# A two-layer hybrid trunk on one core: output projection, second norm and first up-projection products written as one order in the FFN's pool

## The chip, the cores and the metric

One Trainium2 chip, one core of it in use. The metric is the device time of one execution in microseconds; three executions of the kernel before gave 2158.92, 2163.03 and 2165.88 us, median 2163.03.

## The reference

640 tokens (512 latent, 128 context) of width 1024 go through two layers in fp32. What the change touches is the place between the two sub-layers:

```python
merged = jnp.sum(gates * proj, axis=2)
mix = merged @ w_out
x = x + gt1 * mix
h = rmsnorm(x, g2n) * (1 + sc2) + sh2
u, val = jnp.split(h @ w_up, 2, axis=-1)
u = dwconv3(u, conv)
x = x + gt2 * ((jax.nn.gelu(u) * val) @ w_down)
```

`w_out` is 1024x1024, `w_up` 1024x5632, `w_down` 2816x1024; shift, scale and gate come from the conditioning vectors, one value per channel for latent and one for context tokens.

## The kernel before

Activations lie transposed: 128 channels on the partitions, 640 tokens along the free axis, in two chunks of 320 (256 latent and 64 context tokens each). Every fp32 factor is split into a rounded part (`hi`, a cast on ScalarE) and a remainder (`lo`, a subtraction on VectorE), and a product is the sum of three matmuls hi·hi, hi·lo, lo·hi. One matmul streams 320 columns.

**Stages and pools.** Each layer is a mixer stage and an FFN stage. Each opens a pool of its own in the same stretch of SBUF, with the tags laid one behind the other in the order of `PLACES` (L32); a tile of the new pool waits only for those tiles of the old one that lie at its addresses. In the mixer's pool the last tags are `pt`, `yc` and `vm`; in the FFN's, `hT` and `wd`.

**Mixer, end.** Three branches (L570) go over eight column blocks each. A block is 48 matmuls of the input projection, 24 of the branch's own, gate and sum on VectorE. In the last branch the sum is split into `yc` (hi) and `vm` (lo): L191. Behind each split `aside` (L562) queues one or two blocks of the modulation vectors (`mod_block`, L203): two loads of 256 KB each into `pt`, `kc` or `vca`, and four dot products on VectorE (L212) that use `yt` as scratch. The loads take `pt`, `kc`, `pt`, `vca` in turn. In layer 0 two such blocks stand behind the last split, in layer 1 one.

**Output projection** (L614, `project`, called at L1075 from inside the mixer's stage): eight blocks of 48 matmuls; a block's weights (512 KB) come by SyncE's queue into `raw` (three buffers) and are split (L168, L169) into `hi` and `lo`. The last three blocks run the first token chunk together and then the second, so that the first chunk's sum of squares (L223) and root (L237) can be taken meanwhile.

**FFN.** The up-projection multiplies 2x2 blocks with seven products instead of eight (`Up`, L752): product p needs combination p of the weight quarters and combination p of the four quarters of the normalized activations. `norm_quarters` (L696) makes all of the latter: pair by pair for the first chunk (`two`, giving products 1 and 2), then the second chunk with products 7 and 6, and at last 5, 3 and 4 (`one`). A pair is two VectorE products with the spread root (L704), one ScalarE and one POOL operation on the latent strips (L710, L708) and two POOL operations on the context strips (L711). Weight quarters are loaded by SyncE (L643, L644) and added up partly by an accumulating DMA that POOL issues (L645); `sums` (L677) does the rest.

**Order.** Products 1 and 2 of the first three up-projection blocks (72 matmuls, L899 to L903) and all of `norm_quarters` stand before the manual schedule: their order on the engines is the scheduler's. From L1017 on TensorE, VectorE and ScalarE run in the order in which the code is written: a list of products `pe`, and behind each slot the work that `at(slot, rank, ...)` put there. The first 15 slots are the other five products of blocks 0, 1 and 2 (180 matmuls); slot 15 is product 1 of block 3, from where each block takes seven products.

Of the kernel before, what the change touches and what calls it, by code (L numbers as in the profile page):

```python
# [59 lines left out]
def hybrid_kernel(ctx: ExitStack, tc: tile.TileContext, a):  # L60
# [635 lines left out]
    def norm_quarters(x, l, which, rb):  # L696

        rbs = rb + rstd(x, 1)

        def raw_pair(c, i):  # L700
            t = big("gs", NG)
            for j in range(2):
                k, o = 2 * i + j, t[:, j * HALF:(j + 1) * HALF]
                nc.vector.tensor_tensor(o, rbs[c][:, :HALF], x[k][:, c * HALF:(c + 1) * HALF], ALU.mult)  # L704
                sh = mod[l][:, (0, 3)[which] * 8 + k, :]
                sc = scale1[l][:, which, k, :]
# [5 lines left out]
            return t  # L712

        def two(t, i, p0, p1):
            hi, lo = (big("hA", 8, F32R) if p0 == 1 else big("hT", 20, F32R) for _ in range(2))
            split(t, hi, lo)
            for j, p in enumerate((p0, p1)):
                out[i][p] = (hi[:, j * HALF:(j + 1) * HALF], lo[:, j * HALF:(j + 1) * HALF])

        def one(src, i, p):  # L720
            t = big("hT", 20, F32R)
            split(src, t[:, :HALF], t[:, HALF:])
            out[i][p] = (t[:, :HALF], t[:, HALF:])

        out = [{} for _ in range(NP)]
        first = []
        for i in range(NP):
            first.append(raw_pair(0, i))
            two(first[i], i, 1, 2)
        second, x76 = [], []  # L730
        for i in range(NP):
            b11, b21 = first[i][:, :HALF], first[i][:, HALF:]
            second.append(raw_pair(1, i))
            b12, b22 = second[i][:, :HALF], second[i][:, HALF:]
            x76.append(big("gs", NG))
            x7, x6 = x76[i][:, :HALF], x76[i][:, HALF:]
            nc.vector.tensor_tensor(x7, b22, b12, ALU.subtract)
# [6 lines left out]
        for i in range(NP):  # L744
            one(second[i][:, HALF:], i, 3)
# [543 lines left out]
```

## Time and profile before

| | us |
|---|---|
| median of three runs | 2163.03 |
| profiled execution | 2161.66 |
| its span | 2159.9 |
| TensorE busy in the span | 2059.6 |
| VectorE busy | 1389.7 |
| ScalarE busy | 824.4 |
| GpSimd (POOL) busy | 160.2 |

The profiled execution's own time is 1.76 us above its span and 1.37 us below the median. All times in rows are microseconds from the span's start unless marked ns. PE is TensorE, DVE VectorE, ACT ScalarE, POOL GpSimd, SP the queue of SyncE. A row's bracket gives the idle time of the engine just before and what ended it. Matmuls overlap: the pitch from one start to the next is what counts, not a matmul's own duration. PEclk is the granted share of TensorE's full clock.

### The profile page before, as it was taken

Reading aid. Unit: us, or ns where it says so; the run is one execution under the profiler, and the core shown is the slowest. Engines: PE = TensorE matmul, PEld = TensorE weight load, DVE = VectorE, ACT = ScalarE, POOL = GpSimd, SP = SyncE. Lnnn points to the kernel's source line nnn. Section 1 sums busy time; section 2 is a strip of 40 time slices with the busy share of each in tenths; the row PEclk is TensorE's granted clock in tenths of the full one; section 3 lists DMA queues with packets and bytes.
Section 4 is the critical chain, followed back from the end, with each engine's and each line's share of the span. In section 5 each row is a group of like instructions: output and inputs, shape, how many; then the busy total and the mean of one; then the engine's idle time right before and its main releaser. Section 6 shows DMA issues by size and latency. Waiting matters only on the chain.

```text
span 2159.9 us, 34811 instructions
## 1 busy us (share of the span) xinstructions
PE 2059.6 (95%) x13752; PEld 1983.4 (92%) x13752; DVE 1389.7 (64%) x2923; ACT 824.4 (38%) x1329; POOL 160.2 (7%) x344
## 2 busy tenths in 40 slices
PE   6999999999977999999989999999999599999997
PEld 4987999999977999999979779999999599999997
DVE  4247458889767677667652664676664785858676
ACT  4245432222335444344442462222222452535352
POOL 1001000000031000000040100000000310101000
PEclk9999999999988999999999999999999799999998
DMA  8241335556524545354232422353442263535332
GB/s 299 74 128 55 107 105 167 170 178 197 176 59 122 132 111 141 89 142 112 74 121 82 120 85 91 119 170 132 136 144 97 67 163 93 158 103 132 100 99 79
DMA packets 104291, 266.08 MB, mean 123 GB/s; under 512 B 11328, under 2 KB 20800, under 8 KB 104128
## 3 DMA queue, kind: packets, MB, share of 16 engines
q1 hardware_dynamic: 92160, 240.79, 33.4%
q0 software_dynamic: 11968, 23.07, 6.9%
q8 instruction: 108, 1.77, 0.3%
q14 instruction: 55, 0.45, 0.1%
HBM read 252.80 MB, written 6.29 MB: 120 GB/s over the span
## 4 chain that ended last, share of the span: by engine, by line
PE 85%; DVE 8%; DMA 2%; POOL 2%; ACT 2%; issue 1%; SPq 0%; DVEq 0%; POOLq 0%; ACTq 0%
PE mm L182 30%; PE b L763 19%; PE b L875 11%; PE m L182 10%; PE b L182 3%; PE ps L763 3%; DMA raw<-in_w_up 1%; PE ps L452 1%; PE ps L463 1%; DVE lo L672 1%; PE m L442 1%; DVE yt L212 1%; DVE lo L169 1%; PE mm L1121 1%; PE mm L386 1%
## 5 line engine op out<-in xcount | busy, mean ns | idle before, releaser
L182 PE MATMUL mm<-h,hi 128*128 128x320 f32 x2272 | 364.7, 314 | 0.0
L182 PEld LDWEIGHTS mm<-h,hi 128*128 128x128 f32 x2272 | 341.9, 190 | 5.8 <-issue 2.4
L763 PE MATMUL b<-hT,hi 128*128 128x320 f32 x1760 | 306.9, 313 | 16.2 <-ACT hT L190 10.5
L168 ACT CAST hi<-raw 128x1024 fp32r<-128x1024 f32 x140 | 146.8, 1049 | 418.0 <-PE mm L182 262.7
L763 PEld LDWEIGHTS b<-hT,hi 128*128 128x128 f32 x1760 | 273.1, 190 | 18.3 <-ACT hT L190 11.4
L169 DVE TENSOR_TENSOR lo<-raw,hi 128x1024 fp32r<-128x1024 f32 x140 | 172.4, 1232 | 141.8 <-PE mm L182 47.9
L212 DVE SCALAR_TENSOR_TENSOR yt<-mraw,cond 128x512 f32<-128x512 f32 x320 | 220.4, 689 | 7.2
L669 ACT CAST hi<-raw 128x1024 fp32r<-128x1024 f32 (+1 forms) x176 | 164.2, 941 | 120.6 <-DVE raw L679 71.7
L672 DVE TENSOR_TENSOR lo<-raw,hi 128x1024 fp32r<-128x1024 f32 (+1 forms) x176 | 189.7, 1085 | 16.1 <-ACT hi L669 16.1
L182 PE MATMUL mm<-h,lo 128*128 128x320 f32 x1136 | 185.3, 312 | 0.0
L763 PE MATMUL b<-hT,lo 128*128 128x320 f32 x880 | 167.6, 313 | 15.1 <-DVE lo L672 15.1
L182 PEld LDWEIGHTS mm<-h,lo 128*128 128x128 f32 x1136 | 169.8, 188 | 2.9 <-issue 1.0
L875 PE MATMUL b<-gs,hi 128*128 128x320 f32 x1088 | 169.3, 309 | 0.0
L875 PEld LDWEIGHTS b<-gs,hi 128*128 128x128 f32 x1088 | 162.0, 188 | 0.0
L605 DVE SCALAR_TENSOR_TENSOR mx<-b,mod,mx 128x256 f32<-128x256 f32 (+1 forms) x256 | 80.5, 377 | 120.5 <-PE b L875 96.5
L763 PEld LDWEIGHTS b<-hT,lo 128*128 128x128 f32 x880 | 140.2, 191 | 16.3 <-DVE lo L672 16.3
L693 ACT COPY sn<-b 128x320 f32<-128x320 f32 x176 | 75.1, 427 | 123.7 <-PE b L763 123.7
L182 PE MATMUL m<-h,hi 128*128 128x320 f32 x672 | 106.7, 314 | 8.9 <-ACT hi L168 5.9
L182 PEld LDWEIGHTS m<-h,hi 128*128 128x128 f32 x672 | 100.9, 190 | 11.2 <-ACT hi L168 6.1
L645 POOL DMA_DIRECT2D raw<-in_w_up x44 | 53.1, 1206 | 683.0 <-DVE raw L679 298.8
L763 PE MATMUL b<-hA,hi 128*128 128x320 f32 x400 | 80.7, 328 | 22.8 <-ACT hi L669 16.6
L831 DVE SCALAR_TENSOR_TENSOR tmp<-tmp,vecs,tmp 128x642 f32<-128x642 f32 x88 | 77.9, 887 | 21.9 <-ACT tmp L826 17.4
(251 smaller groups left out, 3302.6 us busy)
## 6 DMA issues: line engine op xcount, KB each, us to landing
raw<-in_w_in SPq DMA_DIRECT2D x96, 512.0 KB, 3.5
mraw<-in_w_mod SPq DMA_DIRECT2D x160, 256.0 KB, 2.8
raw<-in_w_up SPq DMA_DIRECT2D x44, 768.0 KB, 5.4
raw<-in_w_up SPq DMA_DIRECT2D x48, 512.0 KB, 3.9
raw<-in_w_up POOLq DMA_DIRECT2D x44, 512.0 KB, 6.5
raw<-in_w_branch SPq DMA_DIRECT2D x24, 512.0 KB, 3.5
wd<-in_w_down SPq DMA_DIRECT2D x32, 384.0 KB, 3.2
wd<-in_w_down SPq DMA_DIRECT2D x32, 320.0 KB, 2.8
```

The costliest lines, as they stand in the source:

```text
L168: nc.scalar.copy(hi[:, :c1 - c0], raw[:, c0:c1])
L169: lows[0] = nc.vector.tensor_tensor(lo[:, :c1 - c0], raw[:, c0:c1], hi[:, :c1 - c0].bitcast(F32), ALU.subtract)
L182: nc.tensor.matmul(bank(ps, c)[:, :HALF], lhsT=w, rhs=v[:, c * HALF:(c + 1) * HALF], start=first, stop=last)
L212: nc.vector.scalar_tensor_tensor(scr[:, :512], raw, 1.0, cond[s][:, hf * 512:(hf + 1) * 512], ALU.mult, ALU.mult, accum_out=acc[:, s, hf:h ...
L605: ins = nc.vector.scalar_tensor_tensor(xv, ps[c][:, sl], gt[:, s:s + 1], xv, ALU.mult, ALU.add)
L645: nc.gpsimd.dma_start(raw[:, 1536:2560].rearrange("p (b n) -> p b n", b=2), src[:, 1536:2048].unsqueeze(1).to_broadcast([P, 2, 512]), accu ...
L669: nc.scalar.copy(view(hi), src)
L672: return lambda: nc.vector.tensor_tensor(view(lo), src, view(hi).bitcast(F32), ALU.subtract)
L693: nc.scalar.copy(t, src)
L763: nc.tensor.matmul(o, lhsT=self.ws.w[p][wi][:, k * P:(k + 1) * P], rhs=self.xt[k][p][xi], start=fresh and j == 0 and k == 0, stop=j == 2 a ...
L831: nc.vector.scalar_tensor_tensor(self.cv[:, inner], self.u[:, j:PADW - 2 + j], self.tap(j), self.cv[:, inner], ALU.mult, ALU.add)
L875: nc.tensor.matmul(self.ps[c][:, :HALF], lhsT=self.w[wi][:, k * P:(k + 1) * P], rhs=self.ups[k].g[xi][:, c * HALF:(c + 1) * HALF], start=k ...
```

## The change

The output projection leaves the mixer's stage: `mixer` returns the merged activations and x, and `entry`, called inside the FFN's manual schedule, runs everything from the projection's first block to product 2 of block 2 in one written order. That schedule now also holds POOL. `yc` and `vm` move to the lasting pool, since the projection reads them in the FFN's stage; `hT` shrinks from 20 to 3 buffers, and the up-projection's split activations use `yc` and `vm` too. The projection's weights are loaded into `wd`, two buffers that grow from 768 to 1024 columns. The norm is a class `Quarters`, called pair by pair; 5, 3 and 4 are made inside the product list. The products 1 and 2 of blocks 0 and 1 run interleaved, one pair of channels at a time (`step`). Cut to its core:

```diff
 PLACES = {
     "mixer": (("bm", 1152, 2), ("h", N, 16), ("s", 384, 4), ("kc", 512, 1), ("vca", 512, 1), ("yt", N, 1), ("qk", N, 10),
-              ("g", N, 2), ("raw", 1024, 3), ("hi", 1024, 2), ("lo", 1024, 2), ("pt", 768, 2), ("yc", N, 8), ("vm", N, 9)),
+              ("g", N, 2), ("raw", 1024, 3), ("hi", 1024, 2), ("lo", 1024, 2), ("pt", 768, 2)),
     "ffn": (("s", 320, 6), ("raw", 2560, 2), ("hA", N, 8), ("hi", 1024, 3), ("lo", 1024, 3), ("gs", N, 12), ("hi4", 512, 2),
-            ("lo4", 512, 2), ("hT", N, 20), ("wd", 768, 2)),
+            ("lo4", 512, 2), ("hT", N, 3), ("wd", 1024, 2)),
...
-        if tag == "mx":
+        if tag in ("mx", "yc", "vm"):
...
-    def norm_quarters(x, l, which, rb):
...
+    class Quarters:
...
+        def square(self, k, c):
+            sq = short("sq")
+            nc.scalar.activation(sq, self.x[k][:, c * HALF:(c + 1) * HALF], AF.Square)
+            if self.acc[c] is None:
+                self.acc[c] = sq
+                if c == 0:
+                    warm = sm.tile([P, 1], F32, tag="warm", bufs=1, name=uid("warm"))
+                    nc.scalar.activation(warm, sq[:, 0:1], AF.Sqrt)
+            else:
+                nc.vector.tensor_tensor(self.acc[c], self.acc[c], sq, ALU.add)
...
+        def pair(self, c, i):
+            t = self.b[c][i] = big("gs", NG)
...
+        def hi(self, src, tag, bufs, i, ps):
...
+            nc.scalar.copy(hi, src)
...
+            return lambda: nc.vector.tensor_tensor(lo, src, hi.bitcast(F32), ALU.subtract)
+        def hi12(self, i):
+            self.low12 = self.hi(self.b[0][i], "hA", 8, i, (1, 2))
...
+        def x5(self, i):
+            b11 = self.b[0][i][:, :HALF]
+            nc.vector.tensor_tensor(b11, b11, self.b[1][i][:, :HALF], ALU.subtract)
+            self.hi(b11, "yc", 8, i, (5,))()
...
+    class Wout:
...
+        def load(self):
+            self.raw = own([P, 1024], F32, "wd", 2, "wd")
+            nc.sync.dma_start(self.raw, a["w_out"][self.l, self.m])
+        def split(self):
+            self.w = tuple(own([P, 1024], F32R, t, 3, t) for t in ("hi", "lo"))
+            nc.scalar.copy(self.w[0], self.raw)
+            nc.vector.tensor_tensor(self.w[1], self.raw, self.w[0].bitcast(F32), ALU.subtract)
...
+        def step(self, p, k):
...
-    def feed_forward(l, x, rb):
-        ups = [Up(l, f, f < NLEAD) for f in range(KF)]
-        ups[0].load()
+    def entry(l, x, mh, q, ups):
+        ws = [Wout(l, x, m, mh) for m in range(KD)]
+        u0, u1, u2 = ups[:NLEAD]
+        for w in ws[:2]:
+            w.load()
+        u0.load()
         both = quarters_tile()
         for f in range(1, NLEAD):
             nc.sync.dma_start(both[:, (f - 1) * 1024:f * 1024], a["w_up"][l, f, :, 0:1024])
-        for f in range(NLEAD):
-            ups[f].ws.hi21(both[:, (f - 1) * 1024:f * 1024] if f else None)
-            ups[f].ws.low21()
-        ups[0].ws.sums()
-        ups[0].ws.hi4()
-        ups[0].ws.low4()
-        xt = norm_quarters(x, l, 1, rb)
+        for m in range(NLEAD):
+            ws[m].split()
+            if m + 2 < KD:
+                ws[m + 2].load()
+        def done(m, c=None):
+            ws[m].add((0, 1) if c is None else (c,))
+            for i in (0, 1) if c is None else (c,):
+                q.square(m, i)
+        full = KD - NLEAD
+        for m in range(full):
+            ws[m].go((0, 1))
+            if m:
+                done(m - 1)
+            ws[m + NLEAD].split()
+            if m + 5 < KD:
+                ws[m + 5].load()
+        ws[5].go((0,))
+        done(4)
+        ws[6].go((0,))
+        done(5, 0)
+        ws[7].go((0,))
+        done(6, 0)
+        ws[5].go((1,), 0, 12)
+        done(7, 0)
+        q.sum_squares(0)
+        ws[5].go((1,), 12, 24)
+        q.root()
+        ws[6].go((1,), 0, 6)
+        q.spread(0)
+        done(5, 1)
+        q.pair(0, 0)
+        q.pair(0, 1)
+        ws[6].go((1,), 6, 24)
+        u0.ws.hi21()
+        q.hi12(0)
+        q.low12()
+        u0.ws.low21()
+        q.pair(0, 2)
+        q.hi12(1)
+        q.low12()
+        q.pair(0, 3)
+        ws[7].go((1,))
+        done(6, 1)
+        u1.ws.hi21(both[:, :1024])
+        q.hi12(2)
+        q.low12()
+        u1.ws.low21()
+        q.hi12(3)
+        q.low12()
         for u in ups:
-            u.xt = xt
-        for u in ups[:NLEAD]:
-            u.p1()
-            u.keep1()
-            u.p2()
-            u.gate0()
+            u.xt = q.xt
+        for k in range(NP):
+            for u in (u0, u1):
+                u.step(1, k)
+                u.step(2, k)
+            if k == 0:
+                done(7, 1)
+                u2.ws.hi21(both[:, 1024:2048])
+                u2.ws.low21()
+                u1.load()
+            if k == 1:
+                q.sum_squares(1)
+                q.root()
+                u0.ws.sums()
+            if k == 2:
+                q.spread(1)
+        for k in range(NP):
+            u2.step(1, k)
+            u2.step(2, k)
+        q.pair(1, 0)
+        q.pair(1, 1)
+        u0.keep1()
+        u1.keep1()
+        q.sum76(0)
+        q.pair(1, 2)
+        q.hi76(0)
+        q.low76()
+        q.sum76(1)
+        q.pair(1, 3)
+        q.hi76(1)
+        q.low76()
+        q.sum76(2)
+        u0.ws.hi65()
+        u0.ws.low65()
+        q.hi76(2)
+        q.low76()
+        q.sum76(3)
+        u2.keep1()
+        q.hi76(3)
+        q.low76()
+    def feed_forward(l, x, mh):
+        ups = [Up(l, f, f < NLEAD) for f in range(KF)]
+        q = Quarters(l, x)
...
-                    at(-1, 0, v.load)
-                    for x_ in (u, v):
-                        if x_ is v:
-                            at(-1, 5, x_.ws.sums)
-                        at(-1, 5, x_.ws.hi65)
-                        at(-1, 5, late(x_.ws, "low65"))
-                    at(-1, 5, w.hi37)
-                    at(0, 5, late(w, "low37"))
+                    at(0, 0, v.ws.sums)
+                    at(0, 0, v.ws.hi65)
+                    at(0, 0, late(v.ws, "low65"))
+                    for i in range(NP):
+                        at(0, 1, lambda i=i: q.x5(i))
+                        at(3, 6, lambda i=i: q.x3(i))
+                        at(5, 6, lambda i=i: q.x4(i))
+                    for y_ in ups[:NLEAD]:
+                        at(1, 1, y_.gate0)
+                    at(1, 2, w.hi37)
+                    at(1, 2, late(w, "low37"))
+                    at(2, 6, w.hi4)
+                    at(2, 6, late(w, "low4"))
...
-        with tc.manual_schedule(engines={mybir.EngineType.PE, mybir.EngineType.DVE, mybir.EngineType.Activation}):
+        with tc.manual_schedule(engines={mybir.EngineType.PE, mybir.EngineType.DVE, mybir.EngineType.Activation,
+                                         mybir.EngineType.Pool}):
+            entry(l, x, mh, q, ups)
...
-        x = load_x(xs if l else a["x"])
-        def wout(m, i=0):
-            blk = block(a["w_out"][l, m], spare=SPARE if i >= NW else None)
-            return [cols(blk, k) for k in range(KD)]
-        return x, project(l, x, wout, 2, mh, NLEAD)
+        return load_x(xs if l else a["x"]), mh
...
-            x, rb = mixer(l, x, rb)
+            x, mh = mixer(l, x, rb)
         with Stage("ffn"):
-            rb = feed_forward(l, x, rb)
+            rb = feed_forward(l, x, mh)
```

`Quarters.sum_squares`, `root` and `spread` hold what `rstd` did (six small matmuls, the root, six small matmuls), `pair`, `sum76`, `x3`, `x4` the operations of `norm_quarters`; `Wout.go` issues the same 24 matmuls per chunk as `gemm`, `Wout.add` is `residual`, and `step` issues the three matmuls of one product for one channel pair.

## Rows read from the trace of the kernel before

**Rows 1.** The page, part 1: busy time by engine.

```profile
PE 2059.6 (95%) x13752; PEld 1983.4 (92%) x13752; DVE 1389.7 (64%) x2923; ACT 824.4 (38%) x1329; POOL 160.2 (7%) x344
```

**Rows 2.** Stretches: length, each engine's busy time, PEclk, DMA share, GB/s.

```profile
558.55:617.69 59.14, 58.61 (x398) 57.57 (x396) 29.45 (x67) 14.87 (x27) 0.00 (x0) 1.00 0.29 97
617.69:646.18 28.49, 17.00 (x87) 16.23 (x86) 23.45 (x48) 14.63 (x24) 15.76 (x23) 0.70 0.44 111
646.18:693.56 47.38, 32.55 (x182) 30.90 (x181) 35.67 (x68) 23.80 (x41) 6.71 (x10) 0.78 0.39 108
1620.45:1678.69 58.24, 58.24 (x398) 57.55 (x396) 25.47 (x52) 14.98 (x27) 0.00 (x0) 1.00 0.25 88
1678.69:1707.33 28.64, 17.35 (x87) 16.57 (x86) 23.25 (x49) 14.72 (x24) 15.78 (x23) 0.70 0.43 109
1707.33:1753.65 46.32, 29.80 (x182) 28.16 (x181) 35.67 (x68) 23.80 (x41) 6.34 (x9) 0.85 0.40 111
```

**Rows 3.** Waits of TensorE, 617:694: total us, times, longest.

```profile
PE b L763 <- ACT hi L669: 8.4, 1, 8.4
PE b L763 <- DVE lo L672: 7.6, 2, 7.2
```

**Rows 4.** The chain in order of time: start, us, line, count.

```profile
697.24 10.56 PE b L763 x72
```

**Rows 5.** Timeline, layer 0, last mixer product and after; PE, DVE.

```profile
557.38 1.34 PE L182 MATMUL m<-qk,lo 128*128 128x320 f32 x8
...
563.21 0.71 PE L182 MATMUL mm<-yc,hi 128*128 128x320 f32 x3 [0.38 <-ACT yc L190]
...
563.93 0.69 DVE L212 SCALAR_TENSOR_TENSOR yt<-mraw,cond 128x512 f32<-128x512 f32 x1
...
569.88 0.68 DVE L212 SCALAR_TENSOR_TENSOR yt<-mraw,cond 128x512 f32<-128x512 f32 x1
```

**Rows 6.** DMA issues: count, size of one, us to landing.

```profile
raw<-in_w_up SPq DMA_DIRECT2D x48, 512.0 KB, 3.9
...
raw<-in_w_out SPq DMA_DIRECT2D x16, 512.0 KB, 3.5
```

**Rows 7.** Timeline, layer 1, the same place; PE, DVE.

```profile
1614.58 2.51 PE L182 MATMUL m<-h,lo 128*128 128x320 f32 x16
...
1619.27 1.34 PE L182 MATMUL mm<-qk,lo 128*128 128x320 f32 x8
...
1627.14 0.69 DVE L212 SCALAR_TENSOR_TENSOR yt<-mraw,cond 128x512 f32<-128x512 f32 x1
```

**Rows 8.** Timeline of PE, layer 0's first up-projection products.

```profile
627.87 3.28 PE L763 MATMUL b<-hA,hi 128*128 128x320 f32 x11
...
639.72 1.04 PE L763 MATMUL b<-hA,hi 128*128 128x320 f32 x6
```

**Rows 9.** Groups by line and form, 617:760: busy us, mean ns.

```profile
L672 DVE TENSOR_TENSOR lo<-raw,hi 128x1024 fp32r<-128x1024 f32 x18 | 21.8, 1218 | 0.9 <-ACT hi L669 0.9
...
L704 DVE TENSOR_TENSOR gs<-ps,mx 128x320 f32<-128x320 f32 x16 | 7.6, 481 | 0.0
...
L191 DVE TENSOR_TENSOR hA<-gs,hA 128x640 fp32r<-128x640 f32 x4 | 3.3, 823 | 2.8 <-ACT hA L190 2.8
...
L669 ACT CAST hi<-raw 128x1024 fp32r<-128x1024 f32 x18 | 18.7, 1045 | 10.3 <-DVE raw L679 9.7 <-ACT tmp L836 0.7
...
L190 ACT CAST hA<-gs 128x640 fp32r<-128x640 f32 x4 | 2.9, 720 | 6.5 <-DVE gs L704 4.1 <-POOL gs L711 2.4
```

**Rows 10.** POOL's strips: two single latent ones, then both groups.

```profile
633.72 0.55 POOL L708 TENSOR_SCALAR gs<-gs,scale,mod 128x256 f32<-128x256 f32 x1
...
640.50 1.70 POOL L708 TENSOR_SCALAR gs<-gs,scale,mod 128x256 f32<-128x256 f32 x1 [0.23 <-DVE gs L704]
...
L708 POOL TENSOR_SCALAR gs<-gs,scale,mod 128x256 f32<-128x256 f32 x16 | 17.0, 1062 | 17.0 <-DVE rt L242 15.1 <-DVE gs L704 1.9
...
L711 POOL TENSOR_SCALAR gs<-gs,scale,mod 128x64 f32<-128x64 f32 x32 | 16.5, 520 | 589.6 <-DVE gs L704 589.6
```

More of the change, by code (lines that the diff above doesn't have):

```diff
@@ L711, in raw_pair @@
                 nc.gpsimd.tensor_scalar(o[:, HL:], o[:, HL:], sc[:, 1:2], sh[:, 1:2], ALU.mult, ALU.add)
[L712 to L737, printed above, removed]
-            nc.vector.scalar_tensor_tensor(x6, x7, -1.0, b11, ALU.mult, ALU.subtract)
-            two(x76[i], i, 7, 6)
@@ L740, in norm_quarters @@
-        for i in range(NP):
-            b11, b12 = first[i][:, :HALF], second[i][:, :HALF]
-            nc.vector.tensor_tensor(b11, b11, b12, ALU.subtract)
-            one(b11, i, 5)
-        for i in range(NP):
-            one(second[i][:, HALF:], i, 3)
-        for i in range(NP):
-            b21, x6 = first[i][:, HALF:], x76[i][:, HALF:]
-            nc.vector.scalar_tensor_tensor(b21, x6, -1.0, b21, ALU.mult, ALU.subtract)
-            one(b21, i, 4)
-        return out
+        def hi(self, src, tag, bufs, i, ps):
+            n = HALF * len(ps)
+            if n == HALF:
+                t = big(tag, bufs, F32R)
+                hi, lo = t[:, :HALF], t[:, HALF:]
+            else:
+                hi, lo = big(tag, bufs, F32R), big(tag, bufs, F32R)
+            nc.scalar.copy(hi, src)
+            for j, p in enumerate(ps):
+                self.xt[i][p] = (hi[:, j * HALF:(j + 1) * HALF], lo[:, j * HALF:(j + 1) * HALF])
+            return lambda: nc.vector.tensor_tensor(lo, src, hi.bitcast(F32), ALU.subtract)
@@ new lines, in hybrid_kernel, with __init__, go, add @@
+    class Wout:
+        def __init__(self, l, x, m, mh):
+            self.l, self.x, self.m, self.mh = l, x, m, mh
+        def load(self):
[5 more added lines that the diff above has]
+            nc.vector.tensor_tensor(self.w[1], self.raw, self.w[0].bitcast(F32), ALU.subtract)
+        def go(self, chunks, i0=0, i1=24):
+            if chunks[0] == 0:
+                self.ps = mmps()
+            todo = [(k, wi, xi) for k in range(KD) for wi, xi in ((0, 0), (0, 1))] + [(k, 1, 0) for k in range(KD)]
+            for i in range(i0, i1):
+                k, wi, xi = todo[i]
+                for c in chunks:
+                    nc.tensor.matmul(self.ps[c][:, :HALF], lhsT=self.w[wi][:, k * P:(k + 1) * P],
+                                     rhs=self.mh[k][xi][:, c * HALF:(c + 1) * HALF], start=i == 0, stop=i == 23)
+        def add(self, chunks):
+            residual(self.l, self.x, self.ps, self.m, 2, chunks)
@@ L765, in product @@
                                      skip_group_check=not fresh)
+        def step(self, p, k):
+            if p == 1 and k == 0:
+                self.a, self.c = (t[:, :HALF] for t in mmps())
+                self.q2 = self.c
+            o = self.a if p == 1 else self.c
+            for j, (wi, xi) in enumerate(((0, 0), (1, 0), (0, 1))):
+                nc.tensor.matmul(o, lhsT=self.ws.w[p][wi][:, k * P:(k + 1) * P], rhs=self.xt[k][p][xi],
+                                 start=j == 0 and k == 0, stop=j == 2 and k == NP - 1)
         def load(self):
@@ L1025, in wdown @@
         def wdown(m, i=0):
-            raw = own([P, 768], F32, "wd", 2, "wd")[:, :n * P]
+            raw = own([P, 1024], F32, "wd", 2, "wd")[:, :n * P]
             nc.sync.dma_start(raw, a["w_down"][l, m, :, f0 * P:f1 * P])
@@ L1155, in final @@
     def final(x, rb):
-        ys = [big("hT", 20) for _ in range(KD)]
+        ys = [big("yc", 8) for _ in range(KD)]
         rbs = rb + rstd(x, 1)
```

44 lines of the change are left out of this document (37 added, 7 removed).

## The prediction

> **What bounds the kernel now.** I read the page first. TensorE is busy 95% of the span [rows 1], so a gain must come from the 5% in which it is idle, or from stretches at half clock. The table of stretches shows where both lie: the output projection runs at full clock and without gaps, and behind it come two stretches with TensorE busy 17.00 of 28.49 and 32.55 of 47.38 us at a granted clock of 0.70 and 0.78 [rows 2]. In layer 1 they look the same. The chain of waits in time order gives the pitch: 72 products take 10.56 us, 0.1467 us each [rows 4]. The first stretch holds 72 products (1 and 2 of blocks 0 to 2), the second 180 (the 15 slots up to block 3). At that pitch they need 10.6 and 26.4 us. So layer 0 loses 17.9 + 21.0 = 38.9 us here, and layer 1 (28.64 and 46.32) 38.0. That is all the change can win: 76.9 us, 3.6%.
>
> The list of waits says for whom TensorE waits: casts of weights on ScalarE, remainders on VectorE [rows 3]. VectorE is busy 23.45 and 35.67 us of the two stretches, but only 29.45 of the projection's 59.14 [rows 2]. What VectorE does after the norm's root can't move into the projection, for it needs the projection's result. Only weight splits can.
>
> **The hand-over from the mixer, layer 0.** The projection's first weights now need `wd`. Counted from PLACES, `wd` begins at 29,952 of the FFN's pool (columns), and the mixer's `pt` lies at 30,592 to 32,128, behind the second `lo` buffer (29,568 to 30,592). So the first `wd` buffer waits for the first `pt` buffer, the second for both. Of the last two modulation blocks the loads take `pt`, `kc`, `pt`, `vca` in turn and end on `pt`; they are read by eight dot products queued behind the last split. In the trace these run from 563.93 to 570.56 [rows 5]. The third and fourth read the first `pt` buffer, the last two the second. Two remainders of the projection (1.22 us each, as in rows 9) that VectorE ran ahead of them go away, so I let them begin at 562 (estimate). The fourth ends 2.9 us later, near 565. Then come one load of 512 KB, 3.5 us [rows 6], and a cast, 1.05 us [rows 9]: first product at 569.5. The mixer's last product gives way at 557.38 + 8 x 0.147 = 558.55 [rows 5]. TensorE is idle 11.0 us, where it waits about 0.5 us today (0.38 of it in rows 5): +10.5. Queued behind the waiting load on SP are the second load and the up-projection's; the third projection block needs its weights 14 us later, which covers them. The bounds: nothing, if the buffers fall otherwise, and 14 us, if the first load needs the last dot product too.
>
> After the idle 8.4 us [rows 3] TensorE ran at half clock: 11 products at a pitch of 0.293 [rows 8]; at 639.72 the pitch is 0.147. Between lay 10 us of running, 5 us lost. I take 4.5 (bounds 0 and 5). Layer 0's hand-over: **+15.0**.
>
> **Layer 1.** Only one modulation block stands behind the split, on the second `pt` buffer. The first `wd` load can start when the last input projection has read `lo`, 1614.58 + 2.51 = 1617.1; with 3.5 and 1.05 the first product comes at 1621.7, against 1619.27 + 1.18 = 1620.45 [rows 7]: 1.3 idle. The first remainder needs the scratch tile, free after the last dot product, 1627.14 + 0.69 = 1627.8 less the one remainder (1.1) that leaves VectorE: 1626.7, and 1.22 more. TensorE wants it 32 products (4.7 us) after its start, at 1626.4: 1.5 idle. The second load waits for the same dot product: 1.1. **+3.9**; bounds 0 and 8.
>
> **The projection itself** costs nothing more: 384 products as before. Its sum into x takes four VectorE instructions a block where two did; the half of that stretch in which VectorE is idle [rows 2] hides them.
>
> **First stretch, products 1 and 2.** With the first chunk's root spread, TensorE has 42 projection products left and 6 of block 0: 7.1 us. Block 1's weight cast stands on ScalarE behind pairs 0 to 3. VectorE's order up to there: the sixth block's second chunk 1.6 (estimate), eight products with the root of which four come at once 1.9, remainder 0.8, weight remainder 1.2, two pairs with 1.0 each and one remainder 0.8 between them: 8.3 [rows 9]. The order is rigid, so waits inside count: the first remainder must see POOL through pair 0 (1.06 for the latent strip, 0.52 for each context strip [rows 10]) and a cast of 0.72, some 1.7 us. Then the cast, 1.05: 11.0, so TensorE waits 3.9; and 2.5 more for block 1's own remainder. With 12 small matmuls (1.6) the stretch takes 10.6 + 6.4 + 1.6 = 18.6 us against 28.5: **-9.9** per layer.
>
> **Second stretch.** From the second root VectorE owes eight root products 3.8, eight sums 3.8, four remainders 3.3, a weight remainder 1.2: 12.1, and about 3.5 of waits in the rigid order, for POOL and ScalarE. On POOL's queue the pairs also stand behind block 1's accumulating DMA, which now waits for its load, 3.9 us [rows 6], after block 2's first remainder; by then the root is nearly spread, so I add nothing (bounds 0 and 4). TensorE has 36 products, 5.3 us, as cover: it waits 10.3. Product 6 of block 1 needs sums, cast and remainder that moved behind the norm: 2.6. Product 7 of block 0 stands behind the four `x5`, each subtraction, cast, subtraction in turn (1.4, so 5.6), a cast and a remainder: 6.7. Snapshots and small waits: 4, as today's tail. 26.4 + 23.6 = 50.0 against 47.4 and 46.3: +2.6 and +3.7. Half clock after these gaps: +3.5 each. Net of both stretches: **-3.8** and **-2.7**.
>
> **Sum.** 15.0 + 3.9 - 3.8 - 2.7 = +12.4 on the profiled execution's 2161.66: 2174.1; with its 1.37 below the median, 2175.4. I forecast **2175 us**.
>
> The price of POOL's strip decides how the pairs run. The single rows show 0.55 us where VectorE multiplied out of PSUM, and 1.70 us where it ran six operations in a row on SBUF operands; the mean is 1.06 [rows 10], which the sum uses. The Trainium skill ("SBUF — State Buffer", section "Who interferes with whom") says that a VectorE instruction with two SBUF inputs and a GpSimd instruction that reads SBUF block each other entirely. That rule speaks against the change, as the new order sets remainders beside every strip; by it all strips would take the long price. What that would be is the second rival.
>
> **Rivals.**
> - *The hand-over is nearly free and the entry holds its gain.* The deciding point is whether the first `wd` load has landed by 558.55. If layer 0 goes as layer 1 does (+3.9 each) and the 15 slots lose no more than today, the time is 2163 + 7.8 - 19.8 = 2151. For it: SP is outside the written order, and the loads may go earlier; VectorE has slack. Against it: the addresses above, and 12 us of norm work on VectorE against 5.3 of cover. 0.26.
> - *POOL's port sets the pace.* Eight strips a layer at 1.70 instead of 1.06 cost 5.1 us per layer if none is hidden: 2185. The six busy operations beside the long strip speak for it, the root products out of PSUM against it. 0.12.
> - *The gains cancel.* Hand-over as summed (+18.9), but the second stretch no longer than today without half clock (-9.9 per layer): 2162. 0.17.
> - The forecast itself: 0.45, by itself 2166 to 2188.
>
> **Numbers.** A measurement of this kernel can tell about 0.3%, 6.5 us, from no change. Slower by more than that is the forecast and the POOL rival: 0.57; within: 0.17; faster: 0.26. The range takes the first rival in at its centre and POOL's at its upper side: 2150 to 2192.
>
> **What would show it.** Right: about 11 us idle of TensorE after the mixer's last product in layer 0, ended by a ScalarE cast of `wd` that waited for DMA, and a granted clock of 0.5 behind it; 1 to 5 us in layer 1; the first stretch near 19 us plus half clock, the second near 50; first waits of product 6 on ScalarE, of product 7 on the cast of 3 and 7. Wrong: no idle time at the hand-over, a second stretch under 40 us, or TensorE waiting for POOL's pairs throughout.

## The result and the profile after

The changed kernel takes 2179.41 us (median of four runs, 2176.61 to 2180.66) against 2161.64 for the kernel before on the same chip: a ratio of 1.0079, 95% interval 1.0058 to 1.0099. It is slower, as forecast, and 4 us above the forecast of 2175. The profiled execution took 2180.01, its span is 2178.2, so 18.3 us more than the span before; the prediction's sum for that difference was 12.4. (The forecast was counted from a median of 2163.03, which with a fourth execution is 2161.64; that is a part of why 2175 looks nearer than the sum is.)

The first row of the page, which answers to [rows 1]: TensorE is busy 95% of the span again, 6.8 us longer for the same number of instructions; in the projections, for one, the granted clock is 0.96 and 0.98 (below) where it was 1.00 [rows 2].

```profile
PE 2066.4 (95%) x13752; PEld 1988.3 (91%) x13752; DVE 1396.2 (64%) x2941; ACT 825.4 (38%) x1325; POOL 151.9 (7%) x344
```

The view of stretches of the changed kernel, with the columns of [rows 2]. Per layer it has four stretches: the gap between the mixer's last product and the projection's first, the projection, the first up-projection stretch (72 products), the second (180).

```profile
559.04:569.77 10.73, 0.00 (x0) 0.00 (x0) 8.69 (x25) 1.77 (x2) 0.00 (x0) 0.73 0.40 119
569.77:629.92 60.15, 60.05 (x397) 59.79 (x398) 28.77 (x61) 18.12 (x28) 3.94 (x7) 0.96 0.38 122
629.92:650.92 21.00, 14.80 (x86) 14.04 (x84) 13.71 (x30) 8.50 (x15) 7.22 (x21) 0.84 0.30 80
650.92:703.36 52.44, 35.95 (x181) 33.11 (x181) 41.10 (x77) 27.54 (x47) 7.35 (x16) 0.80 0.37 101
1630.63:1639.65 9.02, 0.00 (x1) 0.00 (x0) 5.42 (x13) 1.77 (x2) 0.00 (x0) 0.79 0.45 149
1639.65:1699.11 59.46, 59.35 (x397) 59.09 (x397) 28.78 (x61) 18.14 (x28) 3.80 (x7) 0.98 0.36 116
1699.11:1719.74 20.63, 14.64 (x86) 13.77 (x84) 13.61 (x30) 8.24 (x15) 6.96 (x20) 0.83 0.30 78
1719.74:1772.16 52.42, 35.37 (x182) 32.49 (x181) 41.21 (x78) 27.70 (x47) 7.62 (x22) 0.80 0.39 103
```

| us | layer 0 before | forecast | after | layer 1 before | forecast | after |
|---|---|---|---|---|---|---|
| gap at the hand-over | 0.4 | 11.0 | 10.7 | 0 | 3.9 | 9.0 |
| projection | 59.1 | +4.5 (half clock) | 60.2 | 58.2 | +0 | 59.5 |
| first stretch | 28.5 | 18.6 | 21.0 | 28.6 | 18.6 | 20.6 |
| second stretch | 47.4 | 50.0 | 52.4 | 46.3 | 50.0 | 52.4 |
| half clock of both | in them | +3.5 | in them | in them | +3.5 | in them |
| layer, net | | +11.2 | +9.5 | | +1.2 | +8.5 |

The net change runs from the mixer's last product to block 3's first: 134.8 us before in layer 0 (558.72 to 693.56) and 144.3 after, 133.0 (1620.61 to 1753.65) and 141.5 in layer 1. The two make 18.0 of the 18.3 us. Layer 0 came out near what was worked out (its parts less so); of layer 1's 8.5 us only 1.2 were forecast. So the question is what holds the first `wd` load there.

The timeline of the changed kernel around both hand-overs, all engines (L792 loads the projection's weights, L796 casts them, L806 multiplies, L343 loads x):

```profile
564.55 0.69 DVE L212 SCALAR_TENSOR_TENSOR yt<-mraw,cond 128x512 f32<-128x512 f32 x1
565.32 3.37 SPq L792 DMA_DIRECT2D wd<-in_w_out  x2
568.68 1.04 ACT L796 CAST hi<-wd 128x1024 fp32r<-128x1024 f32 x1 [7.09 <-DMA wd<-in_w_out]
569.77 0.90 PE L806 MATMUL b<-yc,hi 128*128 128x320 f32 x2 [10.74 <-ACT hi L796]
...
1623.55 10.88 SPq L343 DMA_DIRECT2D mx<-xs  x2
1633.22 0.83 DVE L191 TENSOR_TENSOR vm<-mx,yc 128x640 fp32r<-128x640 f32 x1 [0.79 <-ACT yc L190]
1634.53 2.67 SPq L792 DMA_DIRECT2D wd<-in_w_out  x2
1639.65 0.90 PE L806 MATMUL b<-yc,hi 128*128 128x320 f32 x2 [9.02 <-ACT hi L796]
```

Layer 0 is the forecast's chain: the fourth dot product (its accumulator is read out at 565.25), the load, the cast, the product at 569.77 (forecast 569.5). In layer 1 none of the dot products ends just ahead of 1634.53. What stands there is SP's own queue: two loads of x, the second of which goes out only after the last split (L191, to 1634.05). The view of SP's waits from 1620 to 1640 (total, times, longest) says the same:

```profile
SPq L343 <- DVE vm L191: 16.6, 2, 10.2
```

In the trace of before, too, this queue holds loads of `w_out` among those of x (SP's rows, layer 1):

```profile
1618.43 4.59 SPq L160 DMA_DIRECT2D raw<-in_w_out  x2
1625.10 0.33 SPq L343 DMA_DIRECT2D mx<-xs  x1
```

TensorE's waits in the changed kernel from 629 to 704, the columns of [rows 3]:

```profile
PE b L823 <- ACT hi L669: 9.2, 2, 5.2
PE b L834 <- ACT hi L669: 4.0, 1, 4.0
PE b L823 <- ACT sn L693: 3.5, 1, 3.5
PE b L823 <- ACT vm L755: 2.9, 2, 2.2
PE b L834 <- DVE lo L672: 2.2, 1, 2.2
PE b L823 <- DVE lo L672: 0.7, 2, 0.4
```

The 6.2 us of L834 (`step`) lie in the first stretch, the other 16.3 in the second. No wait of TensorE is put down to POOL.

### The profile page after: what moved, and what is told of

Read it like the earlier page. It is cut to its first block, busy times and chain, and to the rows that moved or that the text cites. A ratio compares the mean times of both kernels' runs of the same rounds, so it can differ in the third digit from the quotient of the medians.

```text
span 2178.2 us, 34857 instructions
## 1 busy us (share of the span) xinstructions
PE 2066.4 (95%) x13752; PEld 1988.3 (91%) x13752; DVE 1396.2 (64%) x2941; ACT 825.4 (38%) x1325; POOL 151.9 (7%) x344
## 4 chain that ended last, share of the span: by engine, by line
PE 86%; DVE 8%; ACT 3%; issue 1%; DMA 1%; POOL 1%; SPq 0%; DVEq 0%; ACTq 0%; POOLq 0%
PE mm L182 27%; PE b L823 19%; PE b L945 11%; PE m L182 8%; PE b L806 5%; PE b L182 3%; PE ps L823 3%; PE ps L452 1%; PE ps L463 1%; DVE lo L672 1%; PE m L442 1%; DVE yt L212 1%; PE mm L1277 1%; PE mm L387 1%; PE mm L386 1%
## 5 line engine op out<-in xcount | busy, mean ns | idle before, releaser
L182 PE MATMUL mm<-h,hi 128*128 128x320 f32 x2336 | 378.0, 315 | 8.1 <-ACT hi L168 5.9
L168 ACT CAST hi<-raw 128x1024 fp32r<-128x1024 f32 x126 | 132.3, 1051 | 390.5 <-PE mm L182 243.8
L169 DVE TENSOR_TENSOR lo<-raw,hi 128x1024 fp32r<-128x1024 f32 x126 | 153.8, 1221 | 140.7 <-PE mm L182 60.0
L823 PE MATMUL b<-vm,hi 128*128 128x320 f32 x792 | 167.9, 322 | 31.8 <-ACT hi L669 19.0
L605 DVE SCALAR_TENSOR_TENSOR mx<-b,mod,mx 128x256 f32<-128x256 f32 x320 | 101.1, 377 | 129.2 <-PE b L945 96.7
L823 PEld LDWEIGHTS b<-vm,hi 128*128 128x128 f32 x792 | 133.0, 197 | 35.4 <-ACT hi L669 20.5
L645 POOL DMA_DIRECT2D raw<-in_w_up x44 | 53.1, 1207 | 1255.4 <-DVE lo L797 567.5
L823 PE MATMUL b<-yc,hi 128*128 128x320 f32 x704 | 133.2, 312 | 0.0
L823 PEld LDWEIGHTS b<-yc,hi 128*128 128x128 f32 x704 | 112.4, 191 | 0.0
L182 PE MATMUL m<-h,hi 128*128 128x320 f32 x608 | 92.2, 309 | 0.0
L945 PE MATMUL b<-gs,lo 128*128 128x320 f32 x544 | 89.5, 309 | 0.0
```

Of the source, the lines that this page charges most:

```text
L168: nc.scalar.copy(hi[:, :c1 - c0], raw[:, c0:c1])
L169: lows[0] = nc.vector.tensor_tensor(lo[:, :c1 - c0], raw[:, c0:c1], hi[:, :c1 - c0].bitcast(F32), ALU.subtract)
L182: nc.tensor.matmul(bank(ps, c)[:, :HALF], lhsT=w, rhs=v[:, c * HALF:(c + 1) * HALF], start=first, stop=last)
L605: ins = nc.vector.scalar_tensor_tensor(xv, ps[c][:, sl], gt[:, s:s + 1], xv, ALU.mult, ALU.add)
L823: nc.tensor.matmul(o, lhsT=self.ws.w[p][wi][:, k * P:(k + 1) * P], rhs=self.xt[k][p][xi], start=fresh and j == 0 and k == 0, stop=j == 2 a ...
L945: nc.tensor.matmul(self.ps[c][:, :HALF], lhsT=self.w[wi][:, k * P:(k + 1) * P], rhs=self.ups[k].g[xi][:, c * HALF:(c + 1) * HALF], start=k ...
```

## The experiments

Medians of the runs of each kernel and ratios to the kernel before on the same chip (from all runs of both, so they can differ a little from the quotient of the medians). The runs come from several chips, on which the kernel before took 2158.5 to 2161.6, so a difference between two rows of some 2 us says nothing:

| kernel | us | ratio, 95% interval |
|---|---|---|
| e1_x_behind | 2178.26 | 1.0083 (1.0061 to 1.0105) |
| e2_raw_last | 2178.35 | 1.0081 (1.0056 to 1.0106) |
| e3_both | 2170.16 | 1.0052 (1.0034 to 1.0071) |
| e4_strips_scalar | 2181.93 | 1.0102 (1.0083 to 1.0121) |
| e5_first_block | 2158.30 | 0.9996 (0.9987 to 1.0006) |
| e6_entry | 2163.57 | 1.0014 (1.0003 to 1.0025) |
| e7_first_entry | 2151.78 | 0.9964 (0.9947 to 0.9980) |
| e8_deep | 2140.79 | 0.9913 (0.9895 to 0.9932) |
| e9_deep | 2137.87 | 0.9900 (0.9880 to 0.9920) |
| e10_loads | 2124.07 | 0.9837 (0.9819 to 0.9855) |

### What holds the first load: SP's order (e1), the addresses (e2), both (e3)

e1:

```diff
-        return load_x(xs if l else a["x"]), mh
+        return load_x(xs if l else a["x"], range(KD - 1)), mh
...
         for w in ws[:2]:
             w.load()
+        with tc.issue_after(w.ins.ins):
+            x += load_x(xs if l else a["x"], (KD - 1,))
```

> The load of the last x tile, which stands ahead of the first wd load on SP, is put behind the second wd load; addresses as in the changed kernel. Theory A (layer 0's hand-over waits for the fourth of the last dot products through the address, layer 1's for SP's queue: the last x tile's load needs the last split, which ends at 1634.05, and the wd load stands behind it): layer 0 stays at 10.7 us idle; in layer 1 the load goes at about 1627.2, and the first product comes behind the cast of the last merged block (1632.46 + 0.72) and its own cast of 1.04, near 1634.3: idle 3.6 instead of 9.0. With part of the half clock, 5 to 7 us less in all. Theory B (the last dot products gate the load in both layers): no change, 0 +- 2. Theory C (the first product waits for the split of the last merged block, not for weights): no change.

e2:

```diff
-              ("g", N, 2), ("raw", 1024, 3), ("hi", 1024, 2), ("lo", 1024, 2), ("pt", 768, 2)),
+              ("g", N, 2), ("pt", 768, 2), ("hi", 1024, 2), ("lo", 1024, 2), ("raw", 1024, 3)),
```

> In the mixer's pool raw goes to the end and pt ahead of hi, so that wd lies on raw, which is free once the last mixer weights are split; the order on SP stays. Theory A: layer 0's load then goes right behind the last x tile's load (562.52 + 0.4) instead of 565.32, so its idle falls by 2.4 us from 10.7 to 8.3; layer 1 stays at 9.0. In all 2 to 3 us less. Theory B: both loads go as soon as raw is free, ahead of the mixer's end: 10 us less in layer 0, 8 in layer 1. Theory C: no change.

e3 has both edits.

> Both edits together. Theory A: nothing but the modulation loads stands ahead of the wd loads, so they go near 559 in layer 0 and before the mixer's end in layer 1. The cast still stands on ScalarE behind the cast of the last merged block, and in layer 0 the remainder on VectorE behind the eight dot products (to 568.9). Layer 0: first product near 563.7 (4.8 idle) and 1.7 more for the remainder, 6.5 instead of 10.7; layer 1: near 1634.3, 3.6 idle instead of 9.0. With part of the half clock 10 to 13 us less in all. Theory B: no more than the edit of addresses alone, 18 less in both. Theory C: no change.

| gap, us | changed kernel | e1 | e2 | e3 |
|---|---|---|---|---|
| layer 0 | 10.73 | 10.82 | 8.85 | 5.49 |
| layer 1 | 9.02 | 3.55 | 9.25 | 3.54 |
| projection, layer 1 | 59.46 | 65.90 | 60.42 | 59.96 |

Each gap went as theory A said (10.7 and 3.6; 8.3 and 9.0; 4.8 and 3.6) and unlike theory B, for which e1 would have changed nothing and e2 both layers. Only the 1.7 us that e3 was to wait for a remainder in layer 0 did not come: TensorE has no wait in that projection. Two conditions hold the first load in layer 0, the address and behind it SP's queue; in layer 1 the queue alone. Theory C falls with e3. The Trainium skill ("DMA: Bandwidth & Descriptors", section "Anatomy of one DMA — SWDGE (gpsimd) path") says that a DMA's semaphore wait happens on the sequencer that issues it, before dispatch. That agrees with the row at 1623.55, where the wait of one x load holds the `wd` load behind it.

The gaps shrank, but the times hardly moved. e2 was to win 2 to 3 us, which these runs can't tell from nothing (the interval of its ratio is as good as that of the changed kernel). e1 was to win 5 to 7 and won none. The timeline of e1 in layer 1:

```profile
1624.42 10.07 SPq L792 DMA_DIRECT2D wd<-in_w_out  x2
...
1631.46 0.56 PE L806 MATMUL b<-yc,hi 128*128 128x320 f32 x2 [3.55 <-ACT hi L796]
...
1637.03 0.41 SPq L792 DMA_DIRECT2D wd<-in_w_out  x1
...
1649.42 1.04 ACT L796 CAST hi<-wd 128x1024 fp32r<-128x1024 f32 x1 [10.58 <-DMA wd<-in_w_out]
...
1650.51 0.90 PE L806 MATMUL b<-yc,hi 128*128 128x320 f32 x2 [3.17 <-ACT hi L796]
```

The first load went early (1624.42), the second waited for the dot products (its row ends at 1634.5), and the third block's load stood behind it and the 2.25 MB of up-projection weights. It landed 12 us after its issue. The changed kernel covers that, since its TensorE starts 5.5 us later behind the mixer; here it became a gap of 3.2 us with half clock behind it, and the gain was gone: the projection is 6.4 us longer. In e3 both first loads go early, and no such gap is left. Its time fell by 9 us by the medians and by 6 by the ratios, against a forecast of 10 to 13; its six runs lie between 2168.0 and 2178.2.

### POOL's strips on ScalarE (e4)

```diff
-                if j:
+                if j > 1:
                     nc.gpsimd.tensor_scalar(o[:, :HL], ...)
                 else:
                     nc.scalar.activation(o[:, :HL], ...)
```

> The eight latent strips per chunk pair that POOL does are done by ScalarE, like the other eight; everything else as in the changed kernel. Theory A (POOL does not set the pace: its strips take 0.56 us in the first chunk): ScalarE does two strips of 0.60 us in turn per pair, which moves each pair's cast by 0 to 0.5 us; 0 to 4 us more in all. The rival of the prediction (POOL's strips, lengthened by a shared port, set the pace of the pairs): 5 us less per layer, 10 in all.

The first stretch is 21.7 us in both layers against 21.0 and 20.6, the second 52.8 and 53.1 against 52.4: 1 to 2 us per layer more, where the rival wanted 5 less. By itself that is not proof, since the strips' time went to ScalarE instead. The tile view of `gs` on POOL in the changed kernel (shortest, median, longest in ns) tells more. In the first chunk, 624 to 636, not one strip is lengthened:

```profile
L745 POOL TENSOR_SCALAR gs<-gs,scale,mod x8: 384/394/395, 624.7 to 633.5; 128x64 f32<-128x64 f32 x8
L742 POOL TENSOR_SCALAR gs<-gs,scale,mod x4: 555/555/559, 625.1 to 633.0; 128x256 f32<-128x256 f32 x4
```

In the second chunk, 646 to 656, most are:

```profile
L745 POOL TENSOR_SCALAR gs<-gs,scale,mod x8: 392/842/1653, 647.1 to 654.9; 128x64 f32<-128x64 f32 x8
L742 POOL TENSOR_SCALAR gs<-gs,scale,mod x4: 555/958/1600, 647.5 to 654.3; 128x256 f32<-128x256 f32 x4
```

There VectorE waits once for POOL, 1.6 us, TensorE never. So POOL costs the changed kernel no more than about 1.6 us per layer, where the rival had 5.1; it does not set the pace. Why these strips are long is shown in part only: the first of them stand behind block 1's accumulating DMA, which POOL issues at 646.32 (1.2 us), while VectorE is mostly idle; later ones run beside VectorE's sums and remainder.

### The rest of the hand-over (e5)

On top of e3, the first weight block is loaded and split in the mixer's stage, ahead of the written order:

```diff
+        raw = own([P, 1024], F32, "raw", NRAW, "raw")
+        nc.sync.dma_start(raw, a["w_out"][l, 0])
+        for c0, c1 in ((0, 640), (640, 1024)):
+            hi, lo = tmp(F32R, c1 - c0), tmp(F32R, c1 - c0)
+            split(raw[:, c0:c1], hi, lo)
...
-        for w in ws[:2]:
+        for w in ws[1:3]:
             w.load()
```

> On top of e3_both the projection's first weight block is loaded into the mixer's raw and split in the mixer's stage, ahead of the written order (two pieces, into the scratch tiles tmp); the wd loads begin with the second block. Theory A (what is left of the hand-over in e3_both, 5.5 and 3.55 us, is the first block's cast, which stands behind the load and behind the cast of the last merged block): the first product follows the mixer's last one within 0.5 us in both layers, and layer 0 runs without half clock: 9 to 11 us less than e3_both, so about 2160. Rival (the second or third block's weights, whose loads stay where they are, are late next): TensorE waits for them instead, and no more than 4 us are gained.

11.9 us less than e3. The gap is 1.31 and 0.98 us, not 0.5, and its row names VectorE's reading of the mixer's last product:

```profile
562.03 0.57 PE L807 MATMUL b<-yc,tmp 128*128 128x320 f32 x2 [1.32 <-DVE g L588]
```

The projection now takes 58.5 and 58.1 us. With the same entry as the changed kernel, e5 takes the time of the kernel before (interval 0.9987 to 1.0006), and its way from the mixer's last product to block 3 is 132.9 and 133.6 us against 134.8 and 133.0. So the whole loss of the change was its hand-over, and its entry gains little: some 3 us in layer 0 (the two stretches take 73.1 us against 75.9 before), nothing in layer 1 (74.5 against 75.0). The first of these is not won outright: in e5, where the first block's split stands in the mixer, the mixer's last product of layer 0 ends 2.0 us later than before (560.71 against 558.72).

### The entry: weights out of the norm's way (e6), with e5 (e7)

On top of e3, the written order of the entry and the first slots, cut to its core:

```diff
         ws[5].go((0,))
         done(4)
+        u1.ws.hi21_apart(both[:, :1024])
...
         q.hi12(2)
         q.low12()
+        done(7, 1)
+        u2.ws.hi21(both[:, 1024:2048])
-        u1.ws.low21()
         q.hi12(3)
         q.low12()
...
             if k == 1:
                 q.sum_squares(1)
                 q.root()
                 u0.ws.sums()
+                u0.ws.hi65()
+                u0.ws.low65()
...
-                    at(1, 2, w.hi37)
-                    at(1, 2, late(w, "low37"))
+                    at(0, 0, w.hi37)
+                    at(0, 0, late(w, "low37"))
```

> On top of e3_both the order of the entry is changed: block 1's first weights are split during the projection (in the four small tiles hi4, lo4), the last residual and the second sum of squares come before the last two remainders of the first chunk, block 0's sums and its weights for 6 and 5 come ahead of the second root's products, and the weights for 3 and 7 ahead of the four subtractions of 5. Theory A (weights and the last residual, written between the norm's pairs on VectorE and ScalarE, hold up both stretches): the first stretch goes from 21.2 to 13 to 16 us, the second from 52.5 to 43 to 48; 10 to 16 us less per layer, 20 to 32 in all. Rival (the norm's own chain of product, strips, cast and remainder sets the end of both stretches, wherever the weights stand): the waits come back at the next pair, no more than 4 us less per layer.

> Both edits of e5_first_block and e6_entry together on top of e3_both. If they are independent, the sum of their gains: by theory A 29 to 43 us less than e3_both, 2127 to 2141 and so faster than the kernel before; by the rivals 4 to 12 less, 2158 to 2166.

e6 won 6.6 us, 2 to 3 per layer: the rival's size. The first stretch fell from 21.2 to 18.1 and 16.3, missing 13 to 16, and the second did not fall at all (53.0 and 54.8). e7 is 18.4 us faster than e3, nearly the sum of 11.9 and 6.6. It lies between the two bands on record for it, since e5 came out by its theory A and e6 by its rival. It is the first version faster than the kernel before. The weights stood in the way, but not alone. VectorE's timeline in e7 shows the next bound (L742 product with the root, L770 subtraction, L762 remainder):

```profile
634.55 1.68 DVE L742 TENSOR_TENSOR gs<-ps,mx 128x320 f32<-128x320 f32 x4
638.36 0.49 DVE L770 TENSOR_TENSOR gs<-gs 128x320 f32<-128x320 f32 x1 [2.13 <-POOL gs L749]
...
641.14 0.83 DVE L762 TENSOR_TENSOR vm<-gs,vm 128x640 fp32r<-128x640 f32 x1 [0.88 <-ACT vm L759]
...
645.27 0.82 DVE L762 TENSOR_TENSOR vm<-gs,vm 128x640 fp32r<-128x640 f32 x1 [1.53 <-ACT vm L759]
```

At every pair VectorE waits 0.8 to 2.1 us for a strip or a cast that it has just given out, while instructions it could run, such as the next pair's products, stand behind.

### A deeper order (e8, e9), earlier loads (e10)

On top of e7, the same instructions in another order on VectorE, ScalarE and POOL: all products of a chunk first, each remainder one pair behind its cast, block 1's accumulating DMA behind the strips, block 0's sums in the projection, the four subtractions of 5 ahead of their remainders. Cut to its core:

```diff
-        q.pair(1, 0)
-        q.pair(1, 1)
-        q.sum76(0)
-        q.pair(1, 2)
-        q.hi76(0)
-        q.low76()
...
+        for i in range(NP):
+            q.pair(1, i)
+        u1.load_sum()
...
+        for i in range(NP):
+            q.sum76(i)
+            lows.append(q.hi76(i))
...
+            if i:
+                lows[i - 1]()
+        lows[3]()
...
+                    at(1, 1, q.x5s)
                     for i in range(NP):
-                        at(0, 1, lambda i=i: q.x5(i))
```

> On top of e7_first_entry the same VectorE and ScalarE instructions of the norm stand in an order that leaves each one's input time to arrive: all four products of a chunk's pairs ahead of the first remainder, each remainder one pair behind its cast, the four subtractions of 5 (and of 4) ahead of their remainders and behind the snapshots of 6; block 0's sums during the projection; the accumulating DMA of block 1 behind the second chunk's strips on POOL. Theory A (in e7 VectorE is not short of time but waits inside its written order: 0.8 to 2.1 us at each pair for a strip or a cast, and ScalarE's snapshot of 6 stands behind the four casts of 5): first stretch 12 to 14 us instead of 17.8 and 16.7, second 40 to 46 instead of 53.1 and 54.7; 12 to 18 us less per layer, so 2116 to 2130. Rival (VectorE's own work, 14 us busy in the first stretch and 34 in the second, sets the end): no more than 3 us less per layer, 2146 to 2152.

In e8 block 0's sums are formed ahead of the split of its first weights, which reads the same tile, so products 1 and 2 of block 0 use other weights than the reference's; number, form and length of the instructions are the same. It took 11 us less than e7. The first stretch is 13.4 us in both layers, as theory A said. The second, 51.2 and 51.7, missed 40 to 46: VectorE now waits for the loads of block 1's and block 2's quarters instead (3.3 and 6.5 us; total, times, longest from 634 to 690):

```profile
DVE raw L685 <- DMA raw<-in_w_up: 9.9, 2, 6.5
```

e9 sets the sums behind the split.

> The kernel e8_deep with block 0's sums behind the split of its first weights (which reads the same tile) and its weights for 6 and 5 behind the second chunk's strips; nothing else. It should take the time of e8_deep, 2140.8 +- 3: the moved sums (1.4 us of VectorE) stand in the time in which VectorE waits for the second root. A rival would be that they delay the second chunk's products: 2 us more per layer.

It took 2137.87 us, within the 3 us expected. e10 then changes the loads, and with them the places of block 1's sums and of block 0's weights for 4:

```diff
         u0.load()
-        both = quarters_tile()
-        for f in range(1, NLEAD):
-            nc.sync.dma_start(both[:, (f - 1) * 1024:f * 1024], a["w_up"][l, f, :, 0:1024])
+        u1.load()
...
+        first2 = own([P, 1024], F32, "wd", 2, "wd")
+        nc.sync.dma_start(first2, a["w_up"][l, 2, :, 0:1024])
```

> On top of e9_deep the loads: block 1's weights are loaded whole at the start of the projection, into the buffer that held the first weights of blocks 1 and 2, and block 2's first weights into wd when the projection's last block has left it; block 1's sums stand in the projection, block 0's weights for 4 directly behind those for 3 and 7, block 2's load behind that. Theory A (in the deep order the late loads are the next bound: VectorE waits 3.3 us for block 1's and 6.5 us for block 2's quarters, and TensorE behind them 3.2, 3.1, 0.8 and 2.0 us): the second stretch falls from 51 to 42 to 46 us, 10 to 18 us less in all, 2122 to 2131. Rival (VectorE's order of the 15 slots, casts and snapshots on ScalarE, would hold TensorE as long without these loads): less than 3 us per layer, 2135 to 2141. A third way: the larger load at the start delays the projection's fourth block, as in e1_x_behind: a new wait of 2 to 4 us in the projection.

13.8 us less than e9, inside theory A's range (the second stretch went below its 42 to 46), and 1.6% faster than the kernel before (ratio 0.9837, interval 0.9819 to 0.9855). The view of stretches of e10: projection, first and second stretch, both layers.

```profile
561.84:621.68 59.84, 58.51 (x397) 57.82 (x397) 39.40 (x91) 21.54 (x35) 7.79 (x11) 1.00 0.49 148
621.68:635.08 13.40, 12.29 (x86) 11.79 (x84) 10.26 (x23) 7.37 (x13) 7.85 (x15) 1.00 0.11 31
635.08:675.71 40.63, 30.62 (x180) 28.79 (x181) 39.12 (x76) 25.85 (x45) 6.08 (x17) 0.92 0.46 126
1605.12:1663.71 58.59, 58.28 (x396) 57.82 (x397) 36.21 (x80) 21.42 (x35) 7.64 (x11) 1.00 0.43 129
1663.71:1677.10 13.39, 12.28 (x86) 11.78 (x84) 10.26 (x23) 7.38 (x13) 7.85 (x15) 1.00 0.11 31
1677.10:1717.73 40.63, 30.39 (x180) 28.43 (x181) 39.12 (x75) 25.86 (x45) 6.09 (x17) 0.92 0.48 127
```

In the second stretch VectorE is busy 39.12 of 40.63 us: only here does its work, and not its waiting, fill the stretch. The third way showed once, as a gap of 1.0 us in layer 0's projection (59.84 against 58.59): the fourth block's cast waits for its load to 581.22, and TensorE, at 584.26, for the sums into x that stand behind its remainder on VectorE.

## Why the prediction came out as it did

The total is nearer than its parts, and that is luck: +12.4 us were forecast and +18.0 measured between the mixer and block 3, with the hand-over forecast some 3 us too dear in layer 0 and some 6 too cheap in layer 1, and with two errors of 7 to 9 us per layer in the two stretches that all but cancel.

- **Hand-over, layer 0: right.** Address, fourth dot product, load, cast: each at its time, and e2 and e3 show that address and queue together make it. The half clock behind it was mis-sized: 4.5 forecast, measured 60.15 against 58.5 in e5, which has no such gap: 1.6 us. The granted clock was 0.50 for the first 4.4 us of the projection, not for 10. The pitch there is 0.267, not 0.293; the products of [rows 8], too, follow each other at 0.267 once the first (0.41) is out, so that was a misreading.
- **Hand-over, layer 1: the step that failed.** "The first `wd` load can start when the last input projection has read `lo`" looked at the addresses alone. The load also stands on SP's queue behind the last x tile's load, whose buffer is free only after the last split (1634.05). That queue is in the trace of before too, where loads of `w_out` stood among those of x; I placed the moved loads by their addresses and not in SP's order. The runs show 9.0 us of gap instead of 3.9, and 1.2 of half clock: 6.3 us of the 7.3 us by which layer 1 missed. e1, which moves the x load alone, cuts the gap to 3.55.
- **Third block's weights: right, and only just.** "14 us later, which covers them" holds in the changed kernel; e1, which starts 5.5 us sooner, lost its gain exactly there.
- **First stretch: the waits were right, the clock stood in another term.** Forecast 6.4 of waits, measured 6.2 (4.0 for block 1's cast, 2.2 for its remainder; forecast 3.9 and 2.5). What is left of the 21.0, 2.6 us behind the 10.6 and 1.6 of products, is for the most part half clock (granted 0.84), which the forecast held in one term for both stretches.
- **Second stretch and half clock: two errors that cancel.** Waits forecast 23.6, measured 16.3: product 6 waits 8.1, not 10.3; product 7 of block 0 waits 4.4, not 6.7 (the terms named there, 5.6, a cast and a remainder, would even add to 7.9); product 6 of block 1 not at all, not 2.6. Half clock in both stretches was forecast at 3.5 per layer; what the products and the waits leave is 52.44 - 26.4 - 16.3 = 9.7 and 2.6, not all of it half clock. The accumulating DMA on POOL, set at nothing, did cost VectorE something: the second chunk's strips start 1.0 us behind its first product, the first chunk's 0.1, and VectorE waits 1.6 for them. Net of both stretches -2.4 and -1.9 against -3.8 and -2.7.
- **That the rigid order costs waits inside: right, and larger than the cover.** I charged 1.7 and 3.5 us for it per stretch; e8 and e9 show that the order of the same instructions on VectorE, ScalarE and POOL was worth some 7 us per layer (which of the moves in it did how much was not tried), and e10 that the loads were worth as much again behind it.
- **Rivals.** The nearly free hand-over fell to the rows at 565.32 and 1634.53; with it repaired (e5) the time is that of the kernel before, not 2151, so the entry's gain in that rival was too large as well. POOL's port as the pace fell to e4, to first-chunk strips of 0.39 and 0.56 us, and to a wait of 1.6 us in the second. "The gains cancel" fell too: it had the two stretches 9.9 us shorter per layer, and they are 2.4 and 1.9 shorter.

Not tried: the modulation blocks moved ahead of the last split, and what half clock costs by itself, with TensorE kept busy through a gap.

## What to carry to other kernels

When loads move to another stage, place them on their issuing queue as well as in memory: list what stands ahead of them there and what each of those waits for. In these runs the written order cost latency before it cost work: try it with at least one independent instruction between a result given to another engine and the one that reads it back. And when a start becomes earlier, check the third and fourth transfer behind it, not only the first.

## What the runs showed of the hardware

The clock did not always fall in the gap. TensorE's timeline in e3, layer 1, and the view of stretches there (PEclk is the third number from the end):

```profile
1625.99 0.56 PE L806 MATMUL b<-yc,hi 128*128 128x320 f32 x2 [3.55 <-ACT hi L796]
...
1626.98 0.45 PE L806 MATMUL b<-vm,hi 128*128 128x320 f32 x2
1627.27 0.64 PE L806 MATMUL b<-yc,hi 128*128 128x320 f32 x2
1627.71 0.73 PE L806 MATMUL b<-vm,hi 128*128 128x320 f32 x2
1628.25 0.73 PE L806 MATMUL b<-yc,hi 128*128 128x320 f32 x2
```

```profile
1622.45:1625.99 3.54, 0.00 (x0) 0.00 (x0) 2.61 (x4) 1.67 (x2) 0.00 (x0) 1.00 0.00 0
1625.99:1627.37 1.38, 1.38 (x9) 1.38 (x10) 1.31 (x5) 0.00 (x0) 0.00 (x0) 1.00 0.37 45
1627.37:1630.78 3.41, 3.41 (x15) 3.41 (x14) 3.34 (x7) 1.04 (x1) 0.00 (x0) 0.50 0.45 136
```

Through 3.55 us of idling the granted clock stayed at 1.00 (2.4 GHz), and the first products ran at a pitch of 0.147. At 1627.37, with TensorE busy again for 1.4 us, it fell to 0.50 (1.2 GHz) and the pitch to 0.267, for 3.4 us. After the changed kernel's gaps of 10.7 and 9.0 us the clock was at 0.50 when the products began, and the pitch 0.267 behind the first.

A strip that is lengthened by VectorE, which the prediction weighed, is seen best in e8, whose order sets remainders beside strips. POOL's tile view of `gs` in e8, 614 to 626, and VectorE's timeline there:

```profile
L753 POOL TENSOR_SCALAR gs<-gs,scale,mod x8: 388/398/2122, 615.4 to 622.7; 128x64 f32<-128x64 f32 x8
```

```profile
614.82 3.27 DVE L746 TENSOR_TENSOR gs<-ps,mx 128x320 f32<-128x320 f32 x8
618.00 1.24 DVE L674 TENSOR_TENSOR lo<-raw,hi 128x1024 fp32r<-128x1024 f32 x1
619.17 0.85 DVE L766 TENSOR_TENSOR hA<-gs,hA 128x640 fp32r<-128x640 f32 x1
```

While VectorE multiplies out of PSUM (to 618.0) the strips keep 0.39; one that falls beside the two remainders from 618.00 on takes 2.12 us, about as long as both. That agrees with the rule of the Trainium skill ("SBUF — State Buffer", section "Who interferes with whom") that such a pair of instructions locks each other out. The changed kernel's second chunk has such a strip too: the longest, 1.65 us from 651.41 on, beside a remainder and two sums on VectorE (651.66 to 653.43).
